# Two layers of four token mixers on one core: the second layer's merges of A and B and its attention scores as products of rounded parts and remainders

## The chip, the cores and the metric

The kernel runs on one core of one Trainium2 chip. The metric is the device time of one execution in microseconds (us), the median of three runs. The engines are TensorE (in the profile PE for its matmuls and PEld for its weight loads), VectorE (DVE), ScalarE (ACT), GpSimd (POOL) and SyncE (SP), whose queue issues most of the DMAs.

## The reference, cut to what matters

The network has two layers over 256 context and 256 latent tokens of width 2048. Each layer normalises its input, projects it once, and feeds four mixers of width 512: A (windowed attention), B (a bidirectional RWKV scan), C (attention with normalised queries and keys) and D (a bidirectional gated delta rule). The outputs are merged:

```python
def _merge(ys, pm, g_up, g_b, w_br, w_out):
    acc = jax.nn.sigmoid(pm @ g_up[0] + g_b[0]) * (ys[0] @ w_br[0])
    for i in range(1, N_BRANCH):
        acc = acc + jax.nn.sigmoid(pm @ g_up[i] + g_b[i]) * (ys[i] @ w_br[i])
    return acc @ w_out
```

An attention takes `softmax(q k^T / 8) v` for 8 heads of 64 features, whose keys and values are shared by four heads each. In the second layer only the latent tokens leave the layer, so queries, gates and merges have 256 columns there; keys still have 512.

## The kernel before, in words

Features lie on the 128 partitions, tokens along the free dimension, so a product has a 128x128 weight block as its stationary operand and 512 (layer 1) or 256 (layer 2) tokens as its moving one.

A product of two fp32 matrices is done in one of two forms. In the first, each operand is split into a rounded part (type fp32r, `hi`, by a cast on ScalarE) and the remainder (`lo`, a subtraction on VectorE), and the product is three fp32r matmuls, hi by hi, hi by lo and lo by hi (`mm3`, line 379). The weights come by DMA into `wr` and are split into `wh` and `wl` (`weights`, line 370), a tile of 128x512 at a time, which is one 256 KB load, one cast and one subtraction for four weight blocks. In the second form, plain, `wr` is used as it is in an fp32 matmul.

Projections, the output projection and all merges of layer 1 have the first form. The table `PLAIN` (line 180) names the merges that have the second: B and A in layer 2. `STACK` (line 179) does the same for the scores of the attentions: where it is true, the two 64-feature halves of a 128-partition tile are used for the rounded part and the remainder of one head, so that one matmul over 128 partitions takes two of the terms at once, and a score is two fp32r matmuls; where it is false, a score is one fp32 matmul over 64 partitions:

```python
                    if STACK[l]:
                        for e in range(2):
                            s.mm(ps[:, 0:nk], qs[:, h, qo:qo + 128], ks[:, h, e, 0:nk], e == 0, e == 1)
                    else:
                        r = slice(64 * h, 64 * h + 64)
                        s.mm(ps[:, 0:nk], q[r, qo:qo + 128], kT[r, 0:nk])
```

Stacked keys `ks` take four times the memory of the plain copy, and are made by two casts, two subtractions and four copies across partitions on GpSimd (line 577). Stacked queries `qs` take two casts and two subtractions per pair of heads and one more step (`yield`) of the attention's generator.

The work of a layer stands in this order. Mixer B runs first, beside the projections. Then mixer D runs head by head (`mixer_d`): the next head is prepared (`d_prep`: three short convolutions in tiles `cz`, norms, decay tables), an inverse of a triangular 64x64 system per chunk is built by 62 dependent VectorE operations on tiles `it` and `iX`, transposed into `iE` and `iF` (line 725) and finished by small matmuls (`inv_gen`), and the head's states are scanned in four steps (`d_scan`, tiles `dZ`, `vs`, `Sd`, results in `acc`). Attention A and then C run as a side generator (`side_gen`), for four pairs of heads each, and each pair in two halves of 128 queries (score, maximum, exponential, transposes, values, output tile `sg`). A step of it is taken whenever the matmuls of D have booked some cost. All of these matmuls also book cost for the filler: a queue of projections and then merges (`merge_gen`, in the order B, A, and then C and D as they are done), from which pieces are taken in proportion to the booked cost (`small`, line 259). The cost of a matmul is a formula by its shape and type (`mm`, line 282). After that, the order of each engine's instructions is fixed when the program is built. A merge reads its mixer's output `y` and the gate input `G` back from DRAM through SyncE's queue, into tiles `Rb`. Behind the merges stands the output projection.

Tiles come from pools with a number of buffers per name. `BX` (line 206) gives layer 2 two buffers of `cz` and `vtok`; in layer 1 each has one.

Of the kernel before, what the change touches and what calls it, by code (L numbers as in the profile page):

```python
# [175 lines left out]
MODL = (((0, 8, 12),), ())  # L176
NMAIN = 6
MORE = 5
STACK = (True, False)
PLAIN = ('', 'BA')  # L180
SIDE = (2.0, 1.8)
RHO = (((1.75,) * 4, (1.65,) * 4), ((1.8,) * 4, (1.4,) * 4))
QUANT = 2600.0
# [4 lines left out]
class Kern:  # L188
# [14 lines left out]
    BUFS.update(mr=16, Z=3, U=3, S=3, vs=3, dZ=3, Sd=4, Rb=16, po=3, ms=1, wr=5, wh=4, wl=4, QD=3, qg=3, dl=4, vn=2,  # L203
                nb=4, dec=4)

    BX = ({}, dict(vtok=2, cz=2))
    def tl(s, pool, shape, tag, dt=F32):
        b = s.BX[s.l].get(tag, s.BUFS.get(tag))
        return pool.tile(shape, dt, tag=tag, name=s.nm(tag), **({"bufs": b} if b else {}))
# [346 lines left out]
    def attn(s, br, pool):  # L556
# [11 lines left out]
        s.rope(k[:, CTX:], pool)  # L568
        if STACK[l]:

# [20 lines left out]
        for j in range(4):  # L591
# [10 lines left out]
            yield  # L602
            if STACK[l]:

# [6 lines left out]
            for m in range(t0 // 128, 4):  # L611
# [7 lines left out]
                for h in range(2):  # L619
                    ps = s.bank()  # L620
                    if STACK[l]:
                        for e in range(2):
# [733 lines left out]
    def merge_gen(s, l, br, first):  # L1356
        nc = s.nc
        plain = br in PLAIN[l]
        load = s.load_plain if plain else s.load_split
# [263 lines left out]
```

## Time and profile before

| what | value |
|---|---|
| median of 3 runs | 2807.53 us (2801.76 to 2811.86) |
| profiled execution, its time | 2812.09 us |
| profiled execution, its span | 2810.3 us |
| TensorE busy, matmuls | 2667.1 us, 95% |
| TensorE busy, weight loads | 2035.5 us, 72% |
| VectorE busy | 1834.1 us, 65% |
| ScalarE busy | 1277.1 us, 45% |
| mean granted TensorE clock | 0.976 |

Matmuls are pipelined, and a busy share of TensorE is not its share of the peak. The rate of a stretch of matmuls is read from the times at which they start. An fp32 matmul leaves two records in the trace, an fp32r one leaves one. VectorE's busy time is the union of its instructions, which overlap a little.

### The profile page before, as it was taken

To read this page: it belongs to the slowest core of one execution; us is meant where nothing else is said; L and a number is where in the kernel's file an instruction comes from. 1 tells how busy PE (TensorE), PEld (TensorE's weight loads), DVE (VectorE), ACT (ScalarE), POOL (GpSimd) and SP (SyncE) were. 2 spreads that over 40 slices of the span, in tenths; PEclk is the share of its full clock that TensorE was granted. 3 is DMA by queue.
4 is the path that set the end of the run, shared out by engine and by line. 5 is a ranking of instruction groups with operands and counts; after the bars stand their busy time and mean duration, and the time that the engine had idled before them with its cause. 6 is when DMAs were issued, how large, how long until landed. Compare 5 with 4: busy or idle time off the path is not lost. (4 is left out here: it accounts for less than half of the span.)

```text
span 2810.3 us, 52526 instructions
## 1 busy us (share of the span) xinstructions
PE 2667.1 (95%) x19438; PEld 2035.5 (72%) x19438; DVE 1834.1 (65%) x5127; ACT 1277.1 (45%) x2737; POOL 180.0 (6%) x436
## 2 busy tenths in 40 slices
PE   7998999999999998999999999999999999999897
PEld 3666666677787777677787756776777877867897
DVE  4337776775486777866553354867866688678775
ACT  3334433443355555654442244444443356445553
POOL 0000000000000101000000000010100010100000
PEclk9999999999999998999999999999989999999999
DMA  9754243323432323325447886322323543423465
GB/s 340 266 188 139 78 134 107 121 87 97 122 123 68 101 92 99 97 61 161 151 115 261 272 279 204 112 80 63 110 67 94 161 139 100 128 88 93 144 190 160
DMA packets 210049, 385.80 MB, mean 137 GB/s; under 512 B 24640, under 2 KB 37824, under 8 KB 209792
## 3 DMA queue, kind: packets, MB, share of 16 engines
q1 hardware_dynamic: 199872, 351.23, 40.1%
q0 software_dynamic: 9920, 31.20, 3.0%
q8 instruction: 153, 2.51, 0.4%
q14 instruction: 104, 0.85, 0.1%
HBM read 346.95 MB, written 35.39 MB: 136 GB/s over the span
## 5 line engine op out<-in xcount | busy, mean ns | idle before, releaser
L283 PE MATMUL big<-Rb,wh 128*128 128x512 f32 (+1 forms) x3280 | 1097.3, 363 | 14.9 <-ACT Rb L1347 6.2
L375 ACT CAST wh<-wr 128x512 fp32r<-128x512 f32 x712 | 439.0, 620 | 801.3 <-PE big L283 572.3
L283 PE MATMUL big<-Ra,wh 128*128 128x512 f32 (+1 forms) x2128 | 771.9, 363 | 7.6 <-DVE po L315 3.4
L312 DVE TENSOR_TENSOR wl<-wr,wh 128x512 fp32r<-128x512 f32 x712 | 487.0, 687 | 335.3 <-ACT wh L375 299.6
L283 PEld LDWEIGHTS big<-Rb,wh 128*128 128x128 f32 x3280 | 610.8, 191 | 124.1 <-ACT raw L309 10.9
L283 PE MATMUL big<-Ra,wl 128*128 128x512 f32 (+1 forms) x1616 | 592.9, 367 | 5.2 <-DVE wl L312 5.1
L283 PEld LDWEIGHTS big<-Ra,wh 128*128 128x128 f32 x2128 | 405.9, 191 | 83.9 <-issue 9.9
L283 PE MATMUL big<-Rb,wl 128*128 128x512 f32 (+1 forms) x1088 | 379.7, 349 | 0.9 <-DVE wl L312 0.9
L283 PEld LDWEIGHTS big<-Ra,wl 128*128 128x128 f32 x1616 | 308.6, 191 | 51.1 <-DVE wl L312 6.5
L283 PEld LDWEIGHTS big<-Rb,wl 128*128 128x128 f32 x1088 | 207.4, 191 | 25.2 <-DVE wl L312 1.1
L312 DVE TENSOR_TENSOR iX<-iX,it 128x60 f32<-128x60 f32 (+24 forms) x744 | 182.7, 246 | 17.8
L312 DVE TENSOR_TENSOR it<-iB,iX 128x60 f32<-128x60 f32 (+24 forms) x744 | 173.7, 233 | 17.3
L315 DVE SCALAR_TENSOR_TENSOR po<-po,big 128x512 f32<-128x512 f32 (+1 forms) x128 | 70.4, 550 | 76.4 <-PE big L283 73.6
L283 PE MATMUL big<-Rb,wr 128*128 128x256 f32 (+1 forms) x448 | 112.4, 427 | 3.8 <-DVE Ra L315 2.4
L309 ACT ACTIVATE po<-big,gb 128x512 f32<-128x512 f32 (+1 forms) x128 | 74.0, 578 | 68.5 <-PE big L283 52.7
L283 PE MATMUL big<-mr,s 128*32 128x512 f32 x384 | 86.3, 619 | 17.5 <-DVE sqa L312 17.5
L283 PEld LDWEIGHTS big<-Rb,wr 128*128 128x128 f32 (+1 forms) x448 | 72.5, 183 | 25.0 <-issue 9.0
L315 DVE SCALAR_TENSOR_TENSOR cz<-raw,par,cz 128x508 f32<-128x508 f32 (+3 forms) x96 | 67.2, 700 | 6.0 <-ACT cz L309 5.4
L309 ACT ACTIVATE sw<-S,wc 128x64 f32<-128x64 f32 x96 | 33.4, 348 | 82.7 <-DVE S L315 75.3
L632 DVE TENSOR_REDUCE mx<-mx 128x1 f32<-128x512 f32 (+1 forms) x96 | 57.0, 598 | 20.8 <-PE mx L283 19.9
L283 PE MATMUL mx<-pT,avt 128*64 128x128 f32 x640 | 62.1, 292 | 1.5 <-ACT pT L658 1.3
L305 PE MATMUL mx<-cst,pt 128*128 128x128 f32 x320 | 52.9, 286 | 7.8 <-ACT pt L309 7.5
(373 smaller groups left out, 3760.2 us busy)
## 6 DMA issues: line engine op xcount, KB each, us to landing
wr<-in_win SPq DMA_DIRECT2D x440, 256.0 KB, 2.8
mr<-in_wmod SPq DMA_DIRECT2D x320, 256.0 KB, 4.9
wr<-in_wbr SPq DMA_DIRECT2D x128, 256.0 KB, 2.7
wr<-in_wout SPq DMA_DIRECT2D x128, 256.0 KB, 3.1
wr<-in_wmod SPq DMA_DIRECT2D x64, 256.0 KB, 3.8
wr<-in_gup SPq DMA_DIRECT2D x64, 256.0 KB, 2.7
x<-in_xT SPq DMA_DIRECT2D x16, 256.0 KB, 5.4
po<-y SPq DMA_DIRECT2D x16, 256.0 KB, 3.1
```

The source lines that it names most:

```text
L283: s.nc.tensor.matmul(o, l, r, start=start, stop=stop)
L305: s.nc.tensor.transpose(o, i, s.c("id"))
L309: s.nc.scalar.activation(o, i, f, bias=bias, scale=scale, **k)
L312: s.nc.vector.tensor_tensor(o, a, b, op)
L315: s.nc.vector.scalar_tensor_tensor(o, a, sc, b, op0, op1)
L375: s.nc.scalar.copy(hi, raw)
L632: nc.vector.tensor_reduce(mx[:, hc], ps[:, 0:nk], AX.X, ALU.max)
```

## The change

Two tables give layer 2 the forms that layer 1 has, and layer 2 has one buffer of `cz` where it had two:

```diff
-STACK = (True, False)
-PLAIN = ('', 'BA')
+STACK = (True, True)
+PLAIN = ('', '')
...
-    BX = ({}, dict(vtok=2, cz=2))
+    BX = ({}, dict(vtok=2))
```

In the merges of A and B of layer 2, each fp32 matmul becomes three fp32r matmuls, and the 48 weight tiles and the mixers' outputs are split. The gate input `G`, which was loaded once plain and once split, is loaded once. Each score of layer 2 becomes two fp32r matmuls.

Since the booked costs and the steps of the attentions change, the order of the engines changes from the middle of layer 2 on. Three places are shown.

TensorE at the last inversion of mixer D in layer 2, before: `big` are products of a merge (here that of C, with its outputs in `Rb` and its weights in `wh` and `wl`), `iF,iL` the first matmuls after the inversion.

```order
L283 MATMUL big_29415<-Rb_29338,wh_29402 128x256
L283 MATMUL big_29415<-Rb_29339,wh_29402 128x256
L283 MATMUL big_29415<-Rb_29338,wl_29403 128x256
L283 MATMUL big_29442<-Rb_29308,wh_29432 128x256
L283 MATMUL big_29442<-Rb_29309,wh_29432 128x256
L283 MATMUL big_29442<-Rb_29308,wl_29433 128x256
L283 MATMUL mx_28979<-iF_28976,iL_28599 32x32 x16
L283 MATMUL big_29442<-Rb_29314,wh_29432 128x256
```

The same place in the changed kernel: `aq,cm` is the rotation of the queries of attention C's last pair of heads, `ks,qs` are its scores.

```order
L283 MATMUL mx_29193<-aq_29166,cm_23641 128x256
L283 MATMUL big_30075<-Rb_30044,wh_30062 128x256
L283 MATMUL big_30075<-Rb_30045,wh_30062 128x256
L283 MATMUL big_30075<-Rb_30044,wl_30063 128x256
L283 MATMUL mx_29286<-iF_29283,iL_28717 32x32 x7
L283 MATMUL mx_29298<-ks_26987,qs_29272 128x512 x2
L283 MATMUL mx_29286<-iF_29283,iL_28717 32x32 x9
L283 MATMUL mx_29336<-ks_26987,qs_29272 128x512 x2
```

Before, a merge stood around the inversion and attention C was done; now the first half of C's last pair stands there, and of C's merge only a part of the first tile.

VectorE in the last inversion, before: `it` and `iX` are its dependent steps, `wl` a split of weights, `po` and `Ra` the gated sum of a merge.

```order
L312 TENSOR_TENSOR iX_28608<-iX_28608,it_28733 128x18x4
L312 TENSOR_TENSOR wl_29351<-wr_29348,wh_29350 128x512
L312 TENSOR_TENSOR it_28736<-iB_28606,iX_28608 128x68
L315 SCALAR_TENSOR_TENSOR po_29236<-po_29236,big_29238 128x256
L312 TENSOR_TENSOR iX_28608<-iX_28608,it_28736 128x17x4
L312 TENSOR_TENSOR Ra_28316<-Ra_28316,po_29236 128x256
```

And in the changed kernel, at the end of that inversion, with the maximum of a score (L632) behind it:

```order
L312 TENSOR_TENSOR it_29279<-iB_28724,iX_28726 128x8
L312 TENSOR_TENSOR iX_28726<-iX_28726,it_29279 128x8
L723 STREAM_TRANSPOSE iE_29282<-iX_28726 128x32x8
L725 STREAM_TRANSPOSE iF_29283<-iE_29282 128x256
L632 TENSOR_REDUCE mx_29296<-mx_29298 128x1
L315 SCALAR_TENSOR_TENSOR mx_29296<-mx_29296,rq_6857_29188 128x1
```

The merge's operations have left the inversion, and C's softmax follows it.

SyncE's queue in the changed kernel, with the numbers of heads in the names: `y1_2_j` is the output of C's pair j, read for C's merge, and `p1_Dg3` the gate of D's last head.

```order
L457 DMA sg_6915_29450<-p1_Cg3_178 128x256
L1344 DMA po_7071_30042<-y1_2_2_243 128x256
L1344 DMA po_7074_30048<-y1_2_3_244 128x256
L457 DMA raw_7059_30003<-p1_Dg3_212 128x256
L372 DMA wr_7122_30252<-in_gup 128x512
L372 DMA wr_7125_30258<-in_wbr 128x512
```

The load of the last pair's output stands ahead of D's last gate and of the weights for the merge's later tiles.

## Rows read from the trace of the kernel before

**Rows 1.** The page, busy time of each engine over the span.
```profile
PE 2667.1 (95%) x19438; PEld 2035.5 (72%) x19438; DVE 1834.1 (65%) x5127; ACT 1277.1 (45%) x2737; POOL 180.0 (6%) x436
```

**Rows 2.** Windows between inversions: length, busy time per engine, granted clock, DMA share, GB/s.
```profile
2311.30:2403.80 92.50, 87.06 (x706) 73.15 (x706) 76.23 (x236) 55.42 (x135) 11.60 (x31) 0.96 0.35 111
2403.80:2516.90 113.10, 107.36 (x656) 81.59 (x656) 76.80 (x277) 51.52 (x125) 8.88 (x26) 0.91 0.33 100
2516.90:2550.30 33.40, 32.60 (x275) 24.89 (x275) 22.60 (x81) 17.56 (x42) 5.51 (x16) 1.00 0.34 97
2550.30:2613.40 63.10, 56.78 (x313) 43.01 (x313) 53.57 (x196) 34.80 (x83) 2.68 (x10) 0.95 0.36 109
2613.40:2690.00 76.60, 73.91 (x648) 68.92 (x647) 56.06 (x141) 45.27 (x96) 5.80 (x15) 1.00 0.49 146
```

**Rows 3.** Timeline of TensorE, rounded products: start, us, operation, tiles, [idle before].
```profile
788.88 0.39 PE L283 MATMUL big<-Rb,wh 128*128 128x512 f32 x1
...
795.48 0.39 PE L283 MATMUL big<-Ra,wh 128*128 128x512 f32 x1
...
2394.80 0.28 PE L283 MATMUL big<-Ra,wl 128*128 128x256 f32 x1
...
2401.88 0.28 PE L283 MATMUL big<-Rb,wh 128*128 128x256 f32 x1
2404.45 0.32 PE L283 MATMUL mx<-iF,iL 32*32 32x32 f32 x4 [2.29 <-DVE iF L725]
...
2407.97 0.41 PE L283 MATMUL big<-Ra,wh 128*128 128x256 f32 x1
2408.18 0.41 PE L283 MATMUL big<-Rb,wh 128*128 128x256 f32 x1
```

**Rows 4.** Timeline of TensorE, a score and three unrounded products, each with its successor.
```profile
2531.78 1.12 PE L283 MATMUL mx<-ks,aq 64*128 64x512 f32 x2
2532.84 0.49 PE L283 MATMUL sc<-vb,iR 128*128 128x128 f32 x2
...
2541.48 1.46 PE L283 MATMUL big<-Rb,wr 128*128 128x256 f32 x6
2542.78 0.38 PE L305 MATMUL mx<-cst,rq_y 128*128 128x128 f32 x2
```

**Rows 5.** VectorE's splits by form (mean ns); the last, of keys, min/median/max.
```profile
L312 DVE TENSOR_TENSOR wl<-wr,wh 128x512 fp32r<-128x512 f32 x211 | 143.9, 688 | 55.0 <-ACT wh L375 50.5 <-PE big L283 2.4 <-ACT sw L309 0.5
L312 DVE TENSOR_TENSOR Rb<-po,Rb 128x256 fp32r<-128x256 f32 x10 | 4.1, 420 | 0.8 <-ACT Rb L1347 0.8
...
L312 DVE TENSOR_TENSOR ks<-aq,ks x4: 683/838/993, 747.7 to 1089.3; 64x512 fp32r<-64x512 f32 x4
```

**Rows 6.** Timeline of VectorE, first and last operation of the last inversion.
```profile
2583.99 1.25 DVE L698 STREAM_TRANSPOSE iB<-iG 128x1024 f32<-128x1024 f32 x1 [1.25 <-ACT iG L694]
...
2613.41 0.41 DVE L725 STREAM_TRANSPOSE iF<-iE 128x256 f32<-128x256 f32 x1
```

**Rows 7.** Timeline of TensorE, end of A's merge and start of C's.
```profile
2595.76 5.02 PE L283 MATMUL big<-Rb,wr 128*128 128x256 f32 x22
2603.29 0.84 PE L283 MATMUL big<-Rb,wh 128*128 128x256 f32 x2 [2.50 <-ACT Rb L1347]
```

**Rows 8.** Timeline of VectorE, last half of C's last pair, first maximum and output.
```profile
2588.33 0.69 DVE L632 TENSOR_REDUCE mx<-mx 128x1 f32<-128x512 f32 x1 [0.21 <-PE mx L283]
...
2596.18 0.29 DVE L315 SCALAR_TENSOR_TENSOR sg<-mx,sg 128x128 f32<-128x128 f32 x1
```

**Rows 9.** Windows, unrounded products alone (tile wr): TensorE's busy time and records.
```profile
2516.90:2550.30 33.40, 17.21 (x67) 1.00 0.34 97
2550.30:2613.40 63.10, 29.12 (x117) 0.95 0.36 109
```

**Rows 10.** Window from the last inversion, products in tiles big alone.
```profile
2613.40:2690.00 76.60, 65.42 (x468) 1.00 0.49 146
```

## What is predicted

> **What bounds the kernel now.** I first read the page's line of busy shares [rows 1]: TensorE is busy 95% of the span, VectorE 65%. An average says little here, so I cut the second layer at the moments when VectorE finishes the 62-step triangular inversion of each head of mixer D (tile iF; D0 to D3 at 2311.3, 2403.8, 2516.9 and 2613.4 us), and D2 to D3 once more at the second state update of head 2 (2550.3) [rows 2]. Between 2311 and 2690 TensorE is busy 90 to 98% of each stretch and VectorE 68 to 85%. The timeline shows why TensorE stays busy: mixer D and the two attentions are chains that wait on VectorE and ScalarE, and the products of projections and merges stand between them as filler. At the last inversion, between its start at 2583.99 and its end at 2613.41 [rows 6], TensorE still runs 22 halves of mixer A's merge in one piece (2595.76), then waits 2.50 us and starts the merge of C [rows 7]. So time is set by TensorE's work as long as there is filler, and by the chains once there is none.
>
> **What the change costs and saves on TensorE.** A merge in layer 2 has 16 output tiles with 2+4 products each, so B and A have 192. Unrounded, each is two records of 256 columns; six of them took from 2541.48 to 2542.78, 1.30 us, so one product is 0.43 us [rows 4]. Rounded, it is three products; 59 intervals from 2394.80 to 2401.88 give 0.120 us each, 0.36 us together [rows 3]. Saved: 192 x 0.07 = 13 us. The attentions have 4 x 2 x 2 x 2 = 32 score products. One now holds TensorE from 2531.78 to 2532.84, 1.06 us [rows 4]; in future two of 512 columns at 0.228 us (29 intervals from 788.88 to 795.48 [rows 3]), 0.46 us. Saved: 32 x 0.60 = 19 us, of which some 6 us is the change of form beside it, which may stay: 13 to 19 us. Together TensorE does 26 to 32 us less; I count 26.
>
> **What it adds elsewhere.** 48 more weight tiles are rounded on ScalarE, which has room (it is busy 35 of the 63 us before D3 [rows 2]), and their remainders taken on VectorE: 48 x 0.688 = 33 us [rows 5]. Eight more 256-column splits of y at 0.420 (the two of the gate input stand already) are 3.4 us, four key splits at 0.838 are 3.4 us, 16 query splits (64x256, not in this trace; as wide as the y split, so I take its 0.42, between 0.3 and 0.69) 6.7 us: 46 us on VectorE, all in the second layer. The key halves are then copied to the other partitions on GpSimd, four copies of the key split's size per attention, some 3.4 us by that split's 0.838; the first score of each attention comes that much later. Products of the projections stand beside it, so I count 0 (up to 2, if TensorE comes to that score early). The single buffer cz lets a convolution in D's preparation start only when the normalised tile before it is out; beside filler that is nothing, without filler it lies on the chain.
>
> **What moves.** The order of each engine is fixed when the kernel is built, and it changes with the cost the kernel books for its products and with the one extra step per pair of heads of both attentions. By the built order, filler per stretch goes so (whole products unrounded, single ones rounded):
> D0-D1: 32 of 512 and 320 of 256 columns, now 37 and 390. D1-D2: 64 and 101 unrounded, now 494. D2-D3: 39 and 91 unrounded, now 91. D3-end: 1305, now 1329. The weight splits on VectorE go 29 to 36, 3 to 39, 5 to 9. The fillers of A and B are thus used up early in D2-D3. What is then left without filler is the rest of head 2's scan, the preparation and inversion of head 3, and attention C's last two pairs of heads; and C's last pair now stands behind the last inversion (it was in front), so C's merge, the next filler, cannot finish its first tile before that.
>
> Stretch by stretch, against [rows 2]:
> - Up to D0: 5 fewer 512-column fillers and cheaper scores, 3 us less, a late key copy against it: -1.
> - D0-D1: TensorE gets 70 x 0.12 + 5 x 0.23 = 9.5 us of filler, loses 3.6 to 5 on 9 scores and half a us on values: 87.1 + 5 = 92, at the present 94% share 97 us. +5 (0 to 10).
> - D1-D2: TensorE 107.4 + 59.3 - 7.7 - 43.1 - 5 = 111 of now 113.1; VectorE 76.8 + 36 x 0.688 + some 25 more additions and splits of a merge at 0.42, less 2 of other work: about 110. Two engines that both want 110 us and wait on each other: at the share of the densest VectorE stretch here, 53.57 of 63.1 or 85%, it takes 129, at TensorE's usual 97% 113; I take 121, the middle. +8 (-1 to +17).
> - D2 to 2550.3: TensorE still has 86 of the 91 single products, 10 us, in place of 33 unrounded ones (67 halves [rows 9]), 14 us, and two cheaper scores: 33.4 - 4 - 1 = 28, and VectorE's 22.6 leave room for it; I take 27. -6 (-8 to -3).
> - 2550.3 to D3: TensorE loses 58 products (117 halves [rows 9]), 25 us, and the start of C's merge. But VectorE is 85% busy, and the work that it has in this piece by the new order (summed with the mean durations of its operations, overlaps and all) is 63 us against 66: one more half of a pair in C stands where the merges' additions stood. -3 (-11 to +5; the low end if all of its 9.5 idle us go).
> - After D3: C's last pair takes two halves in series. One half from its maximum at 2588.33 to its output at 2596.18 is 7.9 us; then y goes through DRAM, and after the same output in this trace C's merge got its first product 7.1 us later (2603.29) [rows 7, 8]; what it waited for there was the split of the gate input, which takes the same path, so 7 us for y is an estimate. 2 x 7.9 + 7.1 = 23 us before the merge runs, where today it runs already at D3. In those 23 us head 3's scan and output are done too, which today stand among the merges (73.91 us of TensorE less 65.42 of merges = 9 us up to 2690 [rows 2, 10]), and 14 more products remain: 23 - 9 + 2 = +16 (+4, where C's pair overlaps with itself, to +20).
> Sum: -1 + 5 + 8 - 6 - 3 + 16 = +19 us.
>
> The clock belongs to this. After 2.29 us without work TensorE came back with 256 columns in 0.21 instead of 0.12 us, the lower of its two levels (1.2 GHz), and the stretch has a mean grant of 0.91 [rows 2, 3]. A starved piece of 80 us will show a low grant; the chain's small products get longer by 2 to 4 us there, which is inside the bounds above.
>
> The profiled execution took 2812.09 us (span 2810.3), 4.6 above the median of 2807.53. 2812 + 19 = 2831; on the median's footing 2827.
>
> A rule stands against this change. In the piece before D3 TensorE's records fill 90%, its weight loads 68% (43.01 of 63.1), VectorE 85% [rows 2]. The Trainium skill (Perfetto Trace Analysis, Identifying the Most-Contended Engine) says that matmul busy time doesn't tell how near TensorE is to its limit and that weight-load busy time does, while for VectorE occupancy is a fair measure. By that, VectorE is the contended engine here and the change feeds it; all 46 us would be paid, the third rival below. The trace agrees only in part: up to 2550 VectorE is 68 to 82% busy, and there the records of TensorE say more.
>
> **Rivals.** (1) TensorE's work decides after all: the saving of 26 us comes through, because the filler only stands elsewhere and the chains, freed of 2-us blocks of merge products, run faster. For it: TensorE's 95%, and VectorE's 20 us of idle time in D2-D3. Against it: the starved piece cannot be shorter than its serial parts. 2807.5 - 26 + 2 (late keys) = 2784. It decides if 2550.3-D3 shrinks to 45 us and C's last pair hides behind head 3's scan. (2) It evens out: D1-D2 costs nothing (both engines overlap at 97%), the starved piece loses 8, the tail costs 10: -1 + 2 + 1 - 6 - 8 + 11 = about 0, 2807. (3) VectorE becomes the bound from D0 on: every added us of it is paid, 2807.5 + 46 - 6 (what head D2's piece gives back) = 2848. For it: D1-D2 with 36 more splits; against it: VectorE's 68% there today. It decides if VectorE is above 95% busy from D0 to D3.
>
> **Chances.** Forecast 0.55 (2827, its own range 2813 to 2845), rival 1 0.15, rival 2 0.20, rival 3 0.10. A measurement of this kernel tells about 0.3%, 8 us, from no change. Slower: 0.52 of the forecast and rival 3, 0.62. Same: rival 2 and the low edge of the forecast, 0.21. Faster: rival 1 and a little of rival 2, 0.17. The range leaves out part of rival 1 and of rival 3: 2795 to 2848.
>
> **What would show it.** In the new profile: no unrounded 256-column products, 0.12 us apart in B's and A's merges, about 0.46 us per score; VectorE's busy time up by some 42 us. D1-D2 about 121 us with VectorE near 90%. Then a hole: TensorE below half busy with a lowered clock from about 2555 to 2640, VectorE holding it, and the first full tiles of C's merge some 23 us after the last iF. The forecast is wrong if TensorE stays over 85% busy there, if C's last pair ends before the last inversion, or if the time from D3 to the end is not longer than 196.9 us.

## The result, and the profile after

The changed kernel takes 2870.98 us (median of 4 runs, 2863.75 to 2878.73) against 2805.38 for the kernel before beside it: ratio 1.0226, 95% interval 1.0202 to 1.0250, 65 us slower by the medians. Forecast was slower by 20, range 2795 to 2848: the sign was right, the size was not, and the time lies outside the range.

The profiled execution took 2878.73 us, the highest of the four. The page's line of busy shares, to be set against [rows 1]:

```profile
PE 2675.5 (93%) x19630; PEld 2066.1 (72%) x19630; DVE 1877.4 (65%) x5203; ACT 1315.4 (46%) x2811; POOL 186.6 (6%) x444
```

VectorE has 43 us more, as counted (42). TensorE, which was to have 26 us less, has 8 more. The windows between the inversions of mixer D (the end of each, D0 to D3, is cut at the same operation as in [rows 2]) show, per line, length, busy time of PE, PEld, DVE, ACT and POOL, granted clock, DMA share and GB/s:

```profile
2321.60:2429.60 108.00, 95.61 (x759) 84.87 (x759) 83.11 (x248) 63.60 (x151) 11.92 (x33) 0.90 0.41 122
2429.60:2554.60 125.00, 109.19 (x859) 95.90 (x859) 104.20 (x329) 79.43 (x181) 11.28 (x29) 0.89 0.35 106
2554.60:2654.00 99.40, 59.30 (x462) 47.96 (x460) 75.18 (x273) 46.34 (x113) 8.71 (x26) 0.77 0.16 49
2654.00:2876.70 222.70, 198.84 (x1571) 188.04 (x1571) 140.48 (x307) 108.21 (x215) 5.31 (x16) 0.91 0.49 147
```

Before, these four were 92.5, 113.1, 96.5 and 196.9 us: +15.5, +11.9, +2.9 and +25.8, together 56. The other 10.4 us of this execution lie ahead of mixer B's last inversion in layer 2 (2151.6 after, 2141.2 before), where both built orders are the same; other kernels' profiled executions pass there between 2130.3 and 2149.5, so I take this as scatter of single executions. What the change does is therefore located for 56 of the 65 us.

The hole, in which TensorE starves, in fine windows:

```profile
2570.00:2590.00 20.00, 20.00 (x168) 17.62 (x167) 14.05 (x57) 10.98 (x27) 0.54 (x1) 1.00 0.29 93
2590.00:2605.00 15.00, 3.78 (x14) 2.78 (x13) 9.66 (x39) 2.84 (x7) 0.54 (x1) 0.65 0.15 50
...
2620.00:2635.00 15.00, 4.71 (x28) 3.04 (x28) 12.46 (x43) 9.49 (x23) 1.49 (x7) 0.73 0.04 10
2635.00:2654.00 19.00, 7.13 (x31) 4.81 (x29) 16.36 (x74) 2.45 (x6) 0.59 (x2) 0.50 0.06 21
2654.00:2680.00 26.00, 20.98 (x172) 16.11 (x173) 7.90 (x23) 11.27 (x27) 3.69 (x13) 0.57 0.00 1
```

TensorE falls from full to a quarter at 2590, and the granted clock of the stretches behind it falls to 0.50, its lower level (1.2 GHz). DMAs all but stop (shares of 0.15 down to 0.00). What TensorE waits for between the first inversion and the end (us, times, longest):

```profile
PE big L283 <- ACT Rb L1347: 15.6, 6, 6.0
PE mx L305 <- ACT pt L309: 13.5, 3, 6.9
PE big L283 <- DVE Rb L312: 10.7, 6, 5.9
PE mx L283 <- DVE iF L725: 9.7, 3, 5.5
PE mx L283 <- DVE qs L312: 8.0, 3, 4.5
PE mx L305 <- DVE cz L315: 6.0, 1, 6.0
```

The largest of the same waits before, from its D0 to its end:

```profile
PE mx L283 <- DVE iF L725: 7.2, 3, 4.5
PE big L283 <- ACT Rb L1347: 4.8, 4, 2.5
```

`Rb` are split inputs of merges, `pt` the exponentials of an attention, `qs` split queries. After the last inversion, VectorE shows the two halves of attention C's last pair, from the first maximum (L632) of a half to its output `sg`:

```profile
2653.98 0.45 DVE L725 STREAM_TRANSPOSE iF<-iE 128x256 f32<-128x256 f32 x1
2656.37 0.69 DVE L632 TENSOR_REDUCE mx<-mx 128x1 f32<-128x512 f32 x1 [1.94 <-PE mx L283]
...
2667.82 0.29 DVE L315 SCALAR_TENSOR_TENSOR sg<-mx,sg 128x128 f32<-128x128 f32 x1 [2.87 <-PE mx L283]
2668.97 0.69 DVE L632 TENSOR_REDUCE mx<-mx 128x1 f32<-128x512 f32 x1 [0.86 <-PE mx L283]
...
2682.69 0.29 DVE L315 SCALAR_TENSOR_TENSOR sg<-mx,sg 128x128 f32<-128x128 f32 x1 [2.52 <-PE mx L283]
```

From the start of the first line to that of the last, the halves take 11.5 and 13.7 us, where the half in [rows 8] took 7.9. On TensorE, a rounded product of a merge, then a score of two, at the full clock and in the hole (each with the start of its successor), and the first product of C's merge behind its last pair:

```profile
2455.81 0.28 PE L283 MATMUL big<-Rb,wh 128*128 128x256 f32 x1
2455.93 0.28 PE L283 MATMUL big<-Rb,wl 128*128 128x256 f32 x1
...
2457.93 0.71 PE L283 MATMUL mx<-ks,qs 128*128 128x512 f32 x2
2458.47 0.72 PE L283 MATMUL mx<-cst,raw 128*128 128x1 f32 x6
...
2655.11 1.22 PE L283 MATMUL mx<-ks,qs 128*128 128x512 f32 x2
2656.26 0.74 PE L283 MATMUL mx<-iF,iL 32*32 32x32 f32 x18
...
2687.73 0.36 PE L283 MATMUL big<-Rb,wh 128*128 128x256 f32 x1
```

The product takes 0.12 us, the score 0.54 and then, with a grant of 0.50 from 2654 to 2657 us, 1.15: in the hole its new form costs more than the old one did at the full clock in [rows 4] (1.06).

### The profile page after: what moved, and what is told of

Read it like the earlier page. It is cut to its first block, busy times and chain, and to the rows that moved or that the text cites. A ratio compares the mean times of both kernels' runs of the same rounds, so it can differ in the third digit from the quotient of the medians.

```text
span 2876.7 us, 53145 instructions
## 1 busy us (share of the span) xinstructions
PE 2675.5 (93%) x19630; PEld 2066.1 (72%) x19630; DVE 1877.4 (65%) x5203; ACT 1315.4 (46%) x2811; POOL 186.6 (6%) x444
## 5 line engine op out<-in xcount | busy, mean ns | idle before, releaser
L283 PE MATMUL big<-Rb,wh 128*128 128x512 f32 (+1 forms) x3664 | 1178.6, 357 | 36.1 <-ACT Rb L1347 16.3
L375 ACT CAST wh<-wr 128x512 fp32r<-128x512 f32 x760 | 468.8, 620 | 824.3 <-PE big L283 604.4
L283 PEld LDWEIGHTS big<-Rb,wh 128*128 128x128 f32 x3664 | 674.6, 192 | 149.3 <-ACT Rb L1347 20.6
L312 DVE TENSOR_TENSOR wl<-wr,wh 128x512 fp32r<-128x512 f32 x760 | 520.1, 688 | 335.5 <-ACT wh L375 320.9
L283 PE MATMUL big<-Rb,wl 128*128 128x512 f32 (+1 forms) x1280 | 435.1, 340 | 0.9 <-DVE wl L312 0.9
L283 PEld LDWEIGHTS big<-Rb,wl 128*128 128x128 f32 x1280 | 244.6, 191 | 25.3 <-DVE wl L312 1.1
L283 PE MATMUL mx<-ks,qs 128*128 128x512 f32 (+1 forms) x192 | 67.4, 437 | 11.3 <-DVE qs L312 8.0
L632 DVE TENSOR_REDUCE mx<-mx 128x1 f32<-128x512 f32 (+1 forms) x96 | 56.8, 597 | 21.6 <-PE mx L283 20.6
L305 PEld LDWEIGHTS mx<-cst,pt 128*128 128x128 f32 x320 | 41.3, 156 | 30.4 <-ACT pt L309 27.0
```

Source lines behind the costliest of these rows:

```text
L283: s.nc.tensor.matmul(o, l, r, start=start, stop=stop)
L305: s.nc.tensor.transpose(o, i, s.c("id"))
L312: s.nc.vector.tensor_tensor(o, a, b, op)
L375: s.nc.scalar.copy(hi, raw)
L632: nc.vector.tensor_reduce(mx[:, hc], ps[:, 0:nk], AX.X, ALU.max)
```

## The experiments

The theory after the result (H, for hole): the work of merges and projections that fills TensorE's gaps is used up before attention C is done; the chains of D and C then run alone, at half clock. Rivals: the entries of the merges, that is their first products, wait for their split inputs (E); VectorE's added work is paid (V; V2 where it is asked of a mended kernel); the scores' splits (S) or the single buffer `cz` (Z) hold the chains. Stretches in us, as above; "filler" is what the built order leaves of merge products between D2 and D3, worked out with 0.43 us per unrounded and 0.12 per rounded one; "C late" is how much of C's last pair stands behind the last inversion. The ratio is to the kernel before, run beside each, with its 95% interval.

| kernel | ratio | D0-D1 | D1-D2 | D2-D3 | D3-end | filler | C late |
|---|---|---|---|---|---|---|---|
| before | 1 | 92.5 | 113.1 | 96.5 | 196.9 | 44 | 0 |
| changed | 1.0226 (1.0202-1.0250) | 108.0 | 125.0 | 99.4 | 222.7 | 11 | 1 |
| e1 merges | 1.0071 (1.0043-1.0099) | 93.9 | 130.9 | 101.7 | 190.8 | 28 | 0 |
| e2 scores | 1.0083 (1.0056-1.0109) | 106.0 | 99.3 | 98.5 | 221.3 | 34 | 1 |
| e3 one cz | 1.0080 (1.0049-1.0111) | 102.9 | 111.7 | 110.4 | 192.5 | 29 | 0 |
| e4 no step | 1.0286 (1.0235-1.0337) | 105.2 | 157.0 | 115.2 | 211.0 | 1 | half |
| e5 pace | 1.0187 (1.0167-1.0208) | 106.1 | 143.4 | 107.0 | 191.2 | 11 | 0 |
| e6 two cz | 1.0134 (1.0105-1.0163) | 102.1 | 116.6 | 97.7 | 222.5 | 25 | 1 |
| e7 packed | 1.0198 (1.0173-1.0224) | 108.1 | 125.6 | 98.3 | 219.8 | 8 | 1 |
| e8 both | 1.0103 (1.0073-1.0134) | 101.3 | 132.8 | 99.2 | 188.6 | 19 | 0 |
| e9 no lo | 1.0029 (1.0005-1.0052) | 97.9 | 115.9 | 98.7 | 190.7 | 33 | 0 |
| e10 GpSimd | 1.0154 (1.0102-1.0206) | 98.9 | 147.2 | 105.9 | 190.2 | 32 | 0 |
| e11 scores, mended | 1.0006 (0.9984-1.0028) | 101.4 | 109.5 | 106.4 | 180.6 | 52 | 0 |
| e12 load | 1.0039 (1.0016-1.0062) | 96.3 | 123.5 | 103.3 | 191.0 | 36 | 0 |

One per cent is 28 us. The kernel before took 2805 to 2814 us beside the different runs, so a run is held against its expectation by its ratio, times the 2807.5 us from which the expectations were worked out. The stretches come from one profiled execution of each kernel.

Read down the columns, the ratio follows the filler in the rough: 44 and 52 us of it go with 1 and 1.0006, 1 to 11 us with 1.0187 to 1.0286. In between, 28 to 36 us go with anything from 1.0029 to 1.0154, so the filler of D2-D3 is not the whole answer.

**e1_merges**: the kernel before with `PLAIN = ('', '')`.

> Only the merges of A and B take the rounded form; the scores stay unrounded and both buffers of cz stay. Theory H (the hole: the products that fill gaps are used up before attention C is done, and the chains then run alone): in the built order 234 rounded products are still left between the third and the last inversion (changed kernel: 91) and attention C ends before the last inversion, so there is no hole; the 13 us that TensorE saves stand against a dense stretch before the third inversion: 2800 to 2820 us. Rival E (merge entries: a merge whose inputs are split is entered while its splits are late, and TensorE waits in order): the entries of B and A cost what they cost in the changed kernel, about 20 to 27 us between the first and the third inversion: 2820 to 2835. Rival V (VectorE's added work is paid): 33 + 3 us on VectorE: about 2840.

20 us slower by the ratio: above H, at E's number, and below V's (36 us more would be 1.013, outside the interval). But E's waits aren't there: TensorE waits 8.4 us for Rb from 2150 to 2790 us, against 6.4 in the kernel before:

```profile
PE big L283 <- DVE Rb L312: 4.6, 6, 1.8
PE big L283 <- ACT Rb L1347: 3.8, 5, 1.3
```

The loss lies between D1 and D3:

```profile
2401.20:2532.10 130.90, 120.09 (x892) 101.03 (x892) 103.46 (x341) 80.30 (x183) 9.38 (x27) 0.93 0.38 112
2532.10:2633.80 101.70, 86.22 (x604) 67.65 (x604) 81.24 (x281) 56.74 (x133) 8.24 (x26) 0.80 0.24 77
```

VectorE has 27 us more in the first than [rows 2] show (103.46 against 76.8). And there is a hole after all: the clock of the second is 0.80.

**e2_scores**: the changed kernel with `PLAIN = ('', 'BA')`.

> Only the scores take the rounded form, with one buffer of cz and the extra step of the attentions; the merges of A and B stay unrounded. Theory H: the order still has 42 unrounded products between the third and the last inversion and attention C ends before that inversion, so nothing starves; TensorE saves 13 to 19 us of scores: 2788 to 2805 us. Rival E: no split merge entries, the same 2788 to 2805. Rival S (scores: the splits of queries and keys lie on the attentions' chains and hold TensorE, or the single cz does): slower, 2815 to 2835. Rival V: 13 us more on VectorE, about 2815.

23 us slower, within S. The expectation named the wrong order (42 products left, C in time, which is e3's); the kernel that ran has C's last pair behind the last inversion, and its tail of 221.3 us is that of the changed kernel. So H's number fails here, this run doesn't test its mechanism, and S isn't excluded by it.

**e3_cz1**: the kernel before with

```diff
-    BX = ({}, dict(vtok=2, cz=2))
+    BX = ({}, dict(vtok=2))
```

> The kernel before with one buffer of cz in layer 2 in place of two, nothing else. Theory H and rival E: a convolution waits for the normalised tile before it, beside filler: within 5 us of before, 2802 to 2812. Rival S in the form that the buffer is what holds the preparation of D's heads (6.0 us of waits for cz stand in the changed kernel's trace): 2813 to 2825.

22 us slower by one buffer of 2 KB per partition, against H's number and above that of the buffer's rival (2830 by the ratio, against 2813 to 2825). But TensorE hardly waits for the buffer: 2.2 us between the last two inversions, 2.4 from D0 on. The built order has 64 more products of projections and the first 9 of B's merge before D1, and D2-D3 starves at a mean grant of 0.80:

```profile
2310.10:2413.00 102.90, 97.96 (x778) 82.89 (x778) 79.61 (x240) 57.62 (x139) 12.72 (x34) 0.97 0.41 125
...
2524.70:2635.10 110.40, 85.33 (x545) 64.03 (x544) 78.54 (x270) 52.40 (x124) 8.09 (x26) 0.80 0.25 73
```

In the first window TensorE is busy 97.96 us, 10.9 more than in [rows 2], and the stretch is 10.4 longer: the products moved there are paid one for one. The last is 13.9 longer with 4 us less of TensorE's work.

**e4_noyield**: the changed kernel with

```diff
-                yield
+                if l == 0:
+                    yield
```

behind the query splits (line 609).

> The changed kernel without the extra step of the attentions after the query split (layer 2 only). In the built order attention C is half a pair further at the last inversion (8 value products behind it in place of 16), but only 6 rounded products of the merges are left between the third and the last inversion in place of 91. Theory H, filler as cause: the hole stays or grows by some 10 us, the piece after the last inversion shrinks by one half of a pair, 8 us: 2862 to 2880. If the late attention alone is the cause (its step more per pair): 2815 to 2840.

80 us slower, some 17 more than the changed kernel (the intervals still overlap): an attention that is half a pair earlier shortens the tail by 12 us, and D1 to D3, with no filler left in its second half, grows by 48. This is H, beyond its number (2888 by the ratio, 2902 as measured, against at most 2880): the stretch without filler runs at almost the lower level throughout, 0.54.

```profile
2576.90:2692.10 115.20, 67.60 (x378) 52.77 (x378) 65.74 (x239) 43.63 (x104) 7.23 (x25) 0.54 0.05 17
```

**e5_pace**: the changed kernel with

```diff
-SIDE = (2.0, 1.8)
+SIDE = (2.0, 2.05)
```

> The changed kernel with one number changed: the pace of the attentions beside mixer D in layer 2, from 1.8 to 2.05 steps' worth per booked cost, so that attention C is done before the last inversion although each pair of heads has one step more. Filler in the built order is again used up before the third inversion. Theory H in two parts, the late pair C (tail of 222.7 us after the last inversion) and the used-up filler before it: the tail goes back to 191 to 197 us, 26 to 31 less, and some of it comes back as attention work between the inversions, so 2840 to 2855 us. If the tail is long for another reason (C's merge, more rounded products at the end), it stays near 220 and the time near 2870.

The tail goes back to 191.2, 31 us less, and 26 come back between D1 and D3; 2862.74 us as measured, 8 above H's range, 5 by the ratio. C's late pair explains the tail and little of the time, and that little is not outside the intervals.

**e6_cz2**: the changed kernel with the second buffer back.

```diff
-        QD = [s.tl(pool, [128, 4, 128], "QD")[:, m0:, :] for d in range(2)]
+        QD = [s.tl(pool, [128, 4 - m0, 128], "QD") for d in range(2)]
...
-    BX = ({}, dict(vtok=2))
+    BX = ({}, dict(vtok=2, cz=2))
```

> The changed kernel with the second buffer of cz back; the place for it is found by allocating QD in layer 2 with the half that is used. The built order then keeps 211 rounded products between the third and the last inversion (changed kernel: 91); attention C is as late as in the changed kernel. Theory Z (the single buffer of cz makes the order use its filler early, 20 to 27 us of the 65 as in the kernel before with one buffer): 2843 to 2855 us, with the gain between the first and the third inversion. If the costs don't add (the hole is the same for either reason): 2860 to 2875.

2849.06 us: of 65 us, 26 go (0.0092 of the ratio; by the two intervals some 15 to 36), as Z said.

```profile
2307.40:2409.50 102.10, 92.61 (x748) 82.42 (x748) 79.65 (x243) 62.23 (x148) 11.60 (x31) 0.93 0.37 116
2409.50:2526.10 116.60, 98.39 (x744) 85.22 (x745) 94.22 (x310) 71.02 (x165) 11.80 (x30) 0.87 0.33 100
```

Of this, 6 us lie between D0 and D1, 8 between D1 and D2 and 2 behind them: 16 are located. The rest of this execution's gain lies ahead of D0, nearly all of it where the two orders are the same (2138.9 against 2151.6 at B's last inversion), and is scatter by the reading above. The smaller QD alone leaves the built order of the kernel before as it is.

**e7_pack**: both parts of a merge's input in one Rb tile.

```diff
-        hi = s.tl(s.R, [128, T], "Rb", F32R)[:, 0:n]
-        lo = s.tl(s.R, [128, T], "Rb", F32R)[:, 0:n]
+        hi = s.tl(s.R, [128, T], "Rb", F32R)
+        lo = hi[:, n:] if s.l else s.tl(s.R, [128, T], "Rb", F32R)
+        hi, lo = hi[:, 0:n], lo[:, 0:n]
```

> The changed kernel with the rounded part and the remainder of a merge's input in the two halves of one Rb tile in layer 2, so that a split merge holds 6 Rb tiles in place of 12. Rival E, that the merges' entries wait because the 16 Rb tiles are taken: the waits of merge products for Rb (some 26 us between 2150 and 2790 in the changed kernel) shrink to under 10 and the time to 2850 to 2862. If the entries wait for the splits themselves (ScalarE and VectorE in order): no change, 2863 to 2878.

No change that these intervals tell, and the waits stay:

```profile
PE big L283 <- ACT Rb L1348: 13.3, 5, 5.9
PE big L283 <- DVE Rb L312: 11.4, 6, 5.9
```

The entries don't wait for free tiles.

**e8_cz2_pace**: e6 with the pace of e5.

> Both mends together: the second cz buffer and the pace 2.05. Theory H and Z: what is left is the dense stretch of the merges (18 us between the first and the third inversion in the run of the merges alone, 26 us in all) less the 13 to 19 us that the scores save on TensorE: 2805 to 2830 us. Rival V (VectorE's 46 us of added work is what is paid): still 2845 or more.

2836.4 us, ratio 1.0103: 6 us above the range of H and Z, and below V's 2845. The attention is in time and D2-D3 keeps 161 rounded products, yet D1-D2 takes 132.8 us:

```profile
2402.60:2535.40 132.80, 118.18 (x902) 102.48 (x902) 108.59 (x355) 83.64 (x192) 11.10 (x29) 0.90 0.33 104
2535.40:2634.60 99.20, 70.11 (x532) 58.95 (x532) 76.76 (x271) 53.19 (x126) 8.38 (x26) 0.76 0.19 60
```

**e9_nolo**: e8, with the remainders of B's and A's weights not made.

```diff
+            if l and br in "BA":
...
+                nc.scalar.copy(hi, raw)
+                return hi, hi
```

> The kernel with both mends (second cz buffer, pace 2.05), and the subtractions that make the remainders of B's and A's weights in layer 2 left out: the third product takes the rounded part again, so TensorE does the same number of products and VectorE 48 x 0.688 = 33 us less; the remainders' share of these merges is missing from the output. Theory V2 (after both mends, what is left is VectorE's added work between the first and the last inversion: it is busy there 85 to 95% and the inversions wait for it): most of the 33 us come back, 2800 to 2815 us, with the stretch from the second to the third inversion near 113 us in place of 133. Rival E2 (the splits themselves are late at the merges' entries, and the scores' splits) : 2828 to 2840.

1.0029 against 1.0103, at the upper end of V2: 21 of the 33 us come back, 17 of them in D1-D2. (The expectation puts VectorE at 85 to 95% in e8; the windows above have it at 82 and 77%.)

```profile
2421.20:2537.10 115.90, 101.54 (x790) 88.04 (x790) 83.95 (x302) 75.12 (x176) 10.77 (x30) 0.90 0.33 99
2537.10:2635.80 98.70, 78.93 (x647) 69.69 (x645) 79.65 (x280) 60.71 (x142) 8.13 (x26) 0.88 0.28 84
```

The order moved too (276 products left in D2-D3 in place of 161), so VectorE's time and the place of the filler are not told apart by this run.

**e10_poolsub**: e8, with the 48 subtractions on GpSimd.

```diff
+                nc.gpsimd.tensor_tensor(lo, raw, hi.bitcast(F32), ALU.subtract)
```

> As the run before, but the 48 subtractions are done by GpSimd (busy 6% of the span) and nothing is left out. Theory V2: as without them where GpSimd is fast enough: its copies of 64x512 take 0.87 us, a subtraction of 128x512 with two inputs by estimate 0.9 to 2 us; 2800 to 2820 us. If GpSimd's work slows VectorE or the weights come too late: 2830 or more. Rival E2: 2828 to 2840.

14 us slower than e8 by the ratio, 19 by the medians (2855.7 against 2836.4). The intervals still overlap; what is clear is that V2's gain did not come, though VectorE has that work no longer. GpSimd takes 1.33 us for one, and VectorE's other instructions pay for it: its busy time is 13 us more than in e8 (1882.9 against 1869.5), not 33 less. D1-D2 of this kernel, mean ns of one:

```profile
L1368 POOL TENSOR_TENSOR wl<-wr,wh 128x512 fp32r<-128x512 f32 x35 | 45.9, 1329 | 71.0 <-ACT wh L1366 44.0 <-PE big L283 15.3 <-ACT iR L309 8.8
L312 DVE TENSOR_TENSOR rq_t<-rq_y 128x4 f32<-128x4 f32 x9 | 3.2, 360 | 0.1
L312 DVE TENSOR_TENSOR Ra<-Ra,po 128x256 f32<-128x256 f32 x5 | 3.2, 639 | 0.0
```

The same in e8:

```profile
L312 DVE TENSOR_TENSOR Ra<-Ra,po 128x256 f32<-128x256 f32 x11 | 4.6, 419 | 0.0
...
L312 DVE TENSOR_TENSOR rq_t<-rq_y 128x4 f32<-128x4 f32 x9 | 1.4, 159 | 0.0
```

The means are 0.2 us longer at four columns and at 256. But a mean hides what happens to one. In e10's timeline:

```profile
2432.36 1.27 POOL L1368 TENSOR_TENSOR wl<-wr,wh 128x512 fp32r<-128x512 f32 x1 [0.74 <-ACT wh L1366]
2432.91 0.29 DVE L315 SCALAR_TENSOR_TENSOR sg<-mx,sg 128x128 f32<-128x128 f32 x1 [0.76 <-PE mx L283]
...
2478.04 1.30 POOL L1368 TENSOR_TENSOR wl<-wr,wh 128x512 fp32r<-128x512 f32 x1 [1.65 <-ACT wh L1366]
2478.21 1.14 DVE L315 SCALAR_TENSOR_TENSOR rq_y<-rq_t,rq_y 128x2 f32<-128x2 f32 x1
...
2479.78 0.16 DVE L315 SCALAR_TENSOR_TENSOR rq_y<-rq_t,rq_y 128x2 f32<-128x2 f32 x1
```

An operation on two columns that begins 0.17 us behind GpSimd's subtraction ends with it, after 1.14 us; once the subtraction is over, the same operation takes 0.16. The output `sg`, which reads a product of TensorE, takes its usual 0.29 us beside a subtraction. Of the 14 instructions of VectorE that begin beside such a subtraction in a row of their own (2399 to 2610 us), nine end with it or up to 0.3 us behind it; the five that took their usual time all read a product of TensorE. The Trainium skill (Perfetto Trace Analysis, Optimizing Scalar/DVE Operations) says that GpSimd and VectorE share a read port of the on-chip memory, so that moving work between the two may not help; these rows agree.

**e11_scores2**: e2 with two buffers of cz (and e6's QD) and the pace 2.1.

> Only the scores rounded (merges of A and B unrounded), with two buffers of cz and the pace 2.1, so that attention C is done before the last inversion and the filler in the built order is spread nearly as in the kernel before. Theory H: what made the run of the scores alone slow (2840) was the buffer and the late pair, and TensorE's 13 to 19 us come through: 2788 to 2803 us. Theory V2: VectorE's 13 us more between the inversions take it back: 2803 to 2815. Rival S (splits on the attentions' chains): 2815 or more.

1.0006: neither H's gain nor S's loss, and within what V2 allows. From D0 to the end:

```profile
2312.30:2810.20 497.90, 451.49 (x3439) 397.27 (x3439) 365.65 (x1091) 263.53 (x596) 37.14 (x101) 0.95 0.43 128
```

TensorE's busy time is 10 us less than before (461.6), and the time 497.9 against 499.0: the saving became idle time.

**e12_load**: the kernel before with one subtraction per weight tile of B and A whose result nobody reads.

```diff
+            lo = s.tl(s.wp, shape, "wl", F32R)
+            s.tt(lo, raw, raw, ALU.subtract)
```

> The kernel before, with one more subtraction of 128x512 on VectorE for each of the 48 weight tiles of B's and A's merges, whose result nobody reads: 33 us more on VectorE, the same products and scores. In the built order 57 unrounded products are left between the third and the last inversion (91 before), and 98 rounded (39). Theory V2: the time grows by 15 to 30 us, 2820 to 2840. If VectorE's idle time (32% between the first and the third inversion) takes it: 2803 to 2812.

1.0039, 11 us (4 to 17 by the interval) for 33 us of work whose result nobody waits for: between the two answers. About two thirds of it cost nothing. (The 32% of idle time that the expectation names is that of D1-D2; from D0 to D2 it is 26%.) The order moved here as well (57 unrounded products in D2-D3 in place of 91).

## Why the prediction was wrong

The forecast had +20 from D0 to the end, the profile has +56. Its four terms were short by 10.5 (D0-D1), 3.9 (D1-D2), 11.9 (D2-D3) and 9.8 us (after D3). Up to D0, leaving out the scatter, nothing changed, against a forecast of -1.

**The step that failed first is the one on `cz`**: "beside filler that is nothing". The buffer cost 22 us alone (e3) and gave back 26 when undone in the changed kernel (e6; 16 of them located in the stretches). With the rounding of the merges (27, below) it is one of the two largest pieces of the 65. I priced the wait for the buffer, which is indeed 2 to 6 us of TensorE's time, and not what happens to the order when it is built with that wait: products of projections and merges stand earlier, and are missing two inversions later. I had counted this filler (70 more 256-column products in D0-D1), but put it down to booked costs and to the attentions' extra step. For the booked costs that was wrong too: with the booked rate of layer 2 lowered from 1.4 to 0.8, a kernel that was only built, not run, has 504 and 81 products in D1-D2 and D2-D3, nearly the 494 and 91 of the changed kernel, while one buffer moves them to 380 and 211 (e6). Of e3's 22 us, 10 are the products that moved into D0-D1, paid there one for one. How the 13.9 of its D2-D3 divide between the buffer's wait on the chain and the missing filler, no run separates.

**D2-D3, forecast -9, measured +2.9.** I let the stretch shrink with TensorE's work. TensorE has 59 us of busy time there in place of 89, and the stretch is no shorter. In the table it lies between 96.5 and 115.2 us whatever filler it has, 1 us or 52, and no kernel is shorter than before. In the starved kernels it is therefore not TensorE's work that holds it; that it is the chain of inversion, preparation and attention is the reading left. In the kernel before TensorE is 93% busy there, so both limits lie close together. How short the chain would be at the full clock is not shown, since every starved stretch ran at a lowered grant (0.54 to 0.90). Products moved out of D2-D3 to D0-D2 are thus paid there and not given back here, and none of TensorE's 26 us arrived. For the scores alone e11 shows the same: 10 us less work, no less time.

**D0-D1, forecast +5, measured +15.5.** With two buffers +9.6 (e6), at the upper end of its range: the filler was counted rightly, the entry of B's merge and the late query splits were not (6.5 us for Rb, 4.5 for qs in the changed kernel). e7 rules out full Rb tiles as the reason of such waits. That the splits stand late, behind other work on ScalarE and VectorE, is argued, not shown.

**D1-D2, forecast +8, measured +11.9.** The middle between VectorE's and TensorE's bound was near (121 against 125), in part by luck: VectorE had 104 us in place of 110, and TensorE waited 10 us for Rb and 3.5 for qs, which the forecast had not. Of the merges' cost (27 us from e11 to e8, whose paces differ a little, 20 in e1), 21 go when the remainders' subtractions do (e9), with the order moved.

**After D3, forecast +16, measured +25.8.** The mechanism was right: every kernel whose whole last pair of C comes late has a tail of 219.8 to 222.7 us, half a pair gives 211.0, none 180.6 to 196.9. The size was not. The two halves were taken at 7.9 us from a piece at full clock and took 11.5 and 13.7 at a mean grant of 0.57, while head 3's scan stood among them: the two halves alone are 9.4 us over, of an excess of 10, and the clock had been allowed 2 to 4 us in all. Clock and scan are not told apart. The first full products of C's merge came 34 us after the inversion, not 23.

**Right**: VectorE's added time (43 for 42), the split of a query (0.42 us), rounded products at 0.12 us [rows 3], and the hole, though it opened at 2590 and not at about 2555. None of the three signs of being wrong came. A score took 0.54 us rather than 0.46.

**The rivals.** The first (TensorE's saving comes through) and the second (it evens out) are refuted by the result, the first also by e11. The third was to show in VectorE above 95% busy from D0 to D3; it is at 77, 83 and 76%, and the loss is more than its 40 us. That VectorE's work is paid holds in part: 33 us added alone cost 11 (e12), taken away from the mended kernel they give 21 (e9). It is part of the answer, not the bound.

Undoing things one after the other gives 2871, 2849 (second cz), 2836 (C in time), then 2816 without the rounded merges: in ratios, steps of 26, 9 and 27 us, and 2 us that are left. The second step is not outside its intervals (1.0105 to 1.0163, then 1.0073 to 1.0134). No version here beats the kernel before.

## What to carry to other kernels

Where chains run beside filler, ask of a change first how much filler it leaves for the last chain, and count it from the built order in time, stretch by stretch; a stretch held by a chain gives nothing back when its filler goes. A buffer that is given up to make room is part of the price, even if the trace shows hardly a wait for it (2.4 us here, for 22). A chain's step that is to run without filler should be priced from rows at the lower clock: here the engine that starved was granted 0.50. And a mean of many instructions that is a little longer can be a few that wait long; the timeline tells which.

## What was not expected of the hardware

In e10, VectorE's instructions beside a GpSimd subtraction of 128x512 are not slowed in proportion: nine of 14 waited until it ended, whatever their own size (1.14 us in place of 0.16 at two columns), and the five others, which read a product of TensorE, were not held (0.29 us for `sg`). And a starved TensorE slowed the very chain that starved it: with the grant at 0.50 a score took 1.15 us instead of 0.54, and in e4 the mean grant over 115 us was 0.54.
